# Attention visits on one core: an fp32 mask, one turn for two blocks, small transposes held for the turn, and one fill per visit

## The chip, the cores and the metric

The kernel runs on one core of a Trainium2 chip. The metric is the device time of one execution in microseconds (us). Five engines work side by side: TensorE (PE in the profile; its weight loads are PEld), VectorE (DVE), ScalarE (ACT), GpSimd (POOL) and SyncE (SP), which issues transfers.

## The reference: a decoder trunk of two layers

The input is 512 tokens by 1024 features, float32. Layer 0 mixes by attention, layer 1 by a short gated convolution, and each layer ends in a gated MLP with a causal convolution of width 3 (2816 features). Only the attention of layer 0 matters here. It has 16 heads of 64: eight "forgetting" heads with a softmax, and eight "stick-breaking" heads.

```python
# forgetting heads, per block of 128 queries
logits = q @ k.T * scale + cum_f[query] - cum_f[key]
logits = where(key_pos <= q_pos, logits, -inf)
out    = softmax(logits) @ v
# stick-breaking heads
z       = q @ k.T * scale
later   = reverse_cumsum(where(strict, log_sigmoid(-z), 0)) - itself
out     = where(strict, exp(log_sigmoid(z) + later), 0) @ v
# both: heads concatenated, then o @ w_out, added to the residual
```

Queries and keys are normalized per head (`rms_norm`) before the product.

## The kernel before

Every product of two float32 matrices is made from halves: ScalarE rounds an operand to fp32r (`hi`, a copy), VectorE takes the rest (`lo`), and TensorE adds hi x hi, hi x lo and lo x hi in PSUM (`mm3`, lines 269 to 275). Weights come by DMA into `raw` and are split the same way (lines 250 and 251).

Attention works on eight pairs of heads; pairs 0 to 3 are forgetting heads (`fox`), 4 to 7 stick-breaking. A pair's 512 queries are four blocks of 128, handled in three units: blocks 0 and 1 together, block 2, block 3 (`UNITS`). So there are 24 visits, one per unit, and the loop at the end of the program runs over them (lines 901 to 916). In visit g:

- `logits(g)` puts the scores of unit g in two PSUM banks "b" (line 645; 64-row products, the two heads side by side). For forgetting heads it adds the decay with the rows `dr` and then the causal mask by a product of an identity with a 128 x 128 mask, both bf16 (line 654). Then softmax or the stick-breaking weights follow on VectorE and ScalarE (lines 662 to 668, 683 to 689) and leave the weights `w`.
- if unit g-2 was the last of its pair, `weigh` multiplies that pair's turned weights with the values (line 741) in banks "a".
- `turn` transposes the weights of unit g-1, block by block, on TensorE through the banks "c" (lines 705 and 717), and ScalarE and VectorE split them into `pt` hi and lo (lines 711, 712, 720, 721). There are two banks "c".

Between these steps stands filling work: generators in the list `fillers` that make one `mm3` (or one triple for values) at each step: projections of later queries and keys (`queries_keys`, lines 271 to 273), of values (`values`, lines 527 to 529), and the output projection (`output`, `output_begin`). `fill(us)` adds `us` to a quota and runs fillers until the quota is used up; if there are none, the quota is kept. `need(what)` calls `fill(0.5)` until something later work needs is there.

The planner's clock, `clock`, advances with `spend(us)`: 0.65 per `mm3`, and so on. `after(us, fn)` puts a small piece of work in the list `later`, and `spend` runs it once its time has come, in the middle of whatever is being written. Each pair's queries and keys have three such pieces: `sums` (3.0 after the second projection; 16 small products of line 564 into a bank "c"), `turned_sums` (1.5 later; two transposes of line 572 into the same bank, then the reciprocal root on VectorE) and `rows` (8.0 later; transposes of line 597, four for each of q and k that needs them, each four in a bank "c"; then line 599 multiplies and lines 372 and 373 split). Only then may that pair's scores be made.

The order so written isn't final: a scheduler of the compiler may put a later instruction ahead of one whose buffer isn't free by its own reckoning. Engines then run their instructions in the order that results.

The constants are `PRE` 12.0 (a fill ahead of the loop), `FILL1` 1.5 (behind the scores), `FILL2` 3.3 (behind the turn, shared between blocks) and `BEFORE` 2.0 (once, when the last scores have been made).

Of the kernel before, what the change touches and what calls it, by code (L numbers as in the profile page):

```python
# [17 lines left out]
F32 = mybir.dt.float32  # L18
F32R = mybir.dt.float32r
# [6 lines left out]
P = 128  # L26
S = 512
# [16 lines left out]
ORDER = (1, 0, 1, 1, 1, 1, 3)  # L44
SUMS, FLAT, ROWS = 3.0, 1.5, 8.0
NSUMS, NROWS, LATE = 4.0, 3.0, 7.0
FILL1, FILL2, BEFORE = 1.5, 3.3, 2.0
UNITS = (0, 1), (2,), (3,)
CLASSIC = 3
SHARE = 0.58  # L50
# [3 lines left out]
def trunk(  # L54
# [7 lines left out]
    act, dve, pe, pool = nc.scalar, nc.vector, nc.tensor, nc.gpsimd  # L62
# [10 lines left out]
    def bank(tag):  # L73
        n_ps[0] += 1
        return ps.tile([P, S], F32, tag=tag, name=f"ps{tag}{n_ps[0]}", bufs={"a": 2, "b": 4, "c": 2}[tag])
# [52 lines left out]
    ident16 = begin[:, S - P:S]  # L128
    make_identity(nc, ident16)
    mask = const.tile([P, P], BF16, tag="mask", name="mask")  # L130
# [51 lines left out]

    clock, later, fillers, quota = [0.0], [], [], [0.0]

    def spend(us):
        clock[0] += us
        while later and later[0][0] <= clock[0]:
            later.pop(0)[2]()

# [8 lines left out]
    def fill(us):  # L198
        quota[0] += us
        while quota[0] > 0 and fillers:  # L200
            before = clock[0]
            if next(fillers[0], None) is None:
                fillers.pop(0)
            quota[0] -= clock[0] - before
# [240 lines left out]
    def choose():  # L445

        one = const.tile([P, 4, 4], F32, tag="one", name="one")
        pool.memset(one, 0.0)
        for j in range(4):
            for e in range(2):  # L450
                pool.affine_select(
                    out=one[:, j, :], in_=one[:, j, :], pattern=[[-1, 4]], compare_op=ALU.not_equal,
                    fill=1.0, base=-(e * HD + 4 * j), channel_multiplier=1,
                )
        both = const.tile([P, 2, 4], F32, tag="both", name="both")
        pool.tensor_tensor(both, one[:, 0::2, :], one[:, 1::2, :], op=ALU.add)
        two = const.tile([P, 4, 2], F32, tag="two", name="two")
        pool.tensor_tensor(two, one[:, :, 0:2], one[:, :, 2:4], op=ALU.add)
        by = const.tile([P, 4], F32, tag="by", name="by")
        pool.tensor_tensor(by, two[:, :, 0], two[:, :, 1], op=ALU.add)  # L460
        cols = const.tile([P, 4], F32, tag="cols", name="cols")
        pool.tensor_tensor(cols[:, 0:2], by[:, 0:2], by[:, 2:4], op=ALU.add)
        pool.tensor_tensor(cols[:, 2:4], by[:, 0::2], by[:, 1::2], op=ALU.add)
        pool.tensor_scalar(cols[:, 3:4], cols[:, 3:4], -1.0, None, op0=ALU.mult)
        sel = {n: cols[:, i:i + 1] for i, n in enumerate(("hi", "lo", "q", "-k"))}
        for p in range(4):
            sel["q", p], sel["k", p] = (both[:, i, p:p + 1] for i in range(2))
        return sel
# [71 lines left out]
    def need(what):  # L540
        while what not in done:
            assert fillers
            fill(0.5)
# [75 lines left out]
    def at_once(u):  # L619

        return (slice(0, 2),) if u == 0 else (slice(0, 1), slice(1, 2))

    def logits(p, u):


        fox = p < 4
        need(("qk", p))
        need("decay")
        (k_hi, k_lo), (q_hi, q_lo) = (halves[p][i] for i in range(2))
        bs = UNITS[u]  # L630
        ss = [bank("b") for _ in range(2)]

        parts, at_ = [], 0
        for i, b in enumerate(bs):
            n = (b + 1) * P
            parts.append((b, n, 256 * i, at_))
            at_ += n
            spend((4 if fox else 3) * max(n, 256) * 0.00044 + (0.12 if fox else 0))

        def scores(ql, kl, first, last):  # L640
            for b, n, c, _ in parts:
                wide = max(n, 256)
                for e in range(2):
                    rows = slice(e * HD, (e + 1) * HD)
                    pe.matmul(ss[e][:, c:c + wide], ql[rows, b * P:n], kl[rows, 0:wide], start=first and b == bs[0], stop=last and b == bs[-1])  # L645

        scores(q_hi, k_hi, True, False)
        scores(q_hi, k_lo, False, False)
        scores(q_lo, k_hi, False, not fox)
        if fox:  # L650
            scores(dl[:, p, :], dr, False, False)
            for e in range(2):
                for b, n, c, _ in parts:
                    pe.matmul(ss[e][:, c + b * P:c + n], ident16, mask, start=False, stop=b == bs[-1])
        w = aw.tile([P, 2, S], F32, tag="w", name=f"w{p}{u}", bufs=2)
        own = [w[:, :, a:a + n] for b, n, c, a in parts]
        if fox:
            m = len(bs)
            top, total, inv = (tiny.tile([P, m, 2], F32, tag=f"{t}{m}", name=f"{t}{p}{u}") for t in ("top", "total", "inv"))
            for j, (b, n, c, a) in enumerate(parts):  # L660
                for e in range(2):
                    dve.reduce_max(top[:, j, e:e + 1], ss[e][:, c:c + n], axis=AX.X, negate=True)
                    act.activation(own[j][:, e, :], ss[e][:, c:c + n], AF.Exp, bias=top[:, j, e:e + 1], accum_out=total[:, j, e:e + 1])
            for es in at_once(u):
                dve.reciprocal(inv[:, :, es], total[:, :, es])
                for j in range(m):
                    for e in range(es.start, es.stop):
                        dve.tensor_scalar(own[j][:, e, :], own[j][:, e, :], inv[:, j, e:e + 1], None, op0=ALU.mult)
        else:

            scale = q_scale[p]
            if not rests:
                rests.append(aw.tile([P, 2, S + 1], F32, tag="rest", name="rest", bufs=1))
                pool.memset(rests[0][:, :, S:S + 1], 0.0)
            rest = rests[0]
            if u == 0:
                pool.memset(rest[:, :, P:P + 1], 0.0)
            for es in at_once(u):
                for j, (b, n, c, a) in enumerate(parts):
                    end = P if b == 0 else S  # L680
                    keys = slice(end - n, end)
                    for e in range(es.start, es.stop):
                        act.activation(rest[:, e, keys], ss[e][:, c:c + n], AF.Sigmoid, scale=scale[:, 1, b, e:e + 1])
                        act.activation(own[j][:, e, :], ss[e][:, c:c + n], AF.Sigmoid, scale=scale[:, 0, b, e:e + 1])
                        back = rest[:, e, keys][:, ::-1]
                        dve.tensor_tensor_scan(back, back, begin[:, S - n:S][:, ::-1], 0.0, op0=ALU.mult, op1=ALU.max)  # L686
                for j, (b, n, c, a) in enumerate(parts):
                    end = P if b == 0 else S
                    dve.tensor_tensor(own[j][:, es], own[j][:, es], rest[:, es, end - n + 1:end + 1], op=ALU.mult)
        return [(b, x) for (b, n, c, a), x in zip(parts, own)]  # L690
# [87 lines left out]
    def output_begin():  # L778
        last_w.append([weights(), weights(AHEAD - 1)])
        yield from output_part(range(4), range(2), "b")  # L780
        last_w.append([weights(AHEAD - 1), weights(0)])
        yield from output_part(range(4), (2,), "b")
# [96 lines left out]
    aw = attn.enter_context(tc.tile_pool(name="aw", bufs=2))  # L879
# [4 lines left out]
    o_tiles = {0: mixed(0)}  # L884

    dl = ap_.tile([P, 4, S], F32R, tag="dl", name="dl")
    dr = aw.tile([P, 2, S + 1], F32, tag="rest", name="dr", bufs=1)[:, 0, 0:S].bitcast(F32R)
    sel = choose()
    run(qk0)
    load_small()  # L890
# [7 lines left out]
    units = [(p, u) for p in range(8) for u in range(len(UNITS))]  # L898
    waiting = {}
    fill(PRE)  # L900
    for g in range(len(units) + 2):
        if g < len(units):
            waiting[g] = logits(*units[g])
            fill(FILL1)
        if g == len(units):
            fillers.append(output_begin())
            fill(BEFORE)
        if g >= 2 and units[g - 2][1] == len(UNITS) - 1:
            p = units[g - 2][0]
            weigh(p)  # L910
            if p == 3:
                fillers.append(output(0, residual))
        if 1 <= g <= len(units):
            for b, w in waiting.pop(g - 1):
                turn(units[g - 1][0], b, w)
                fill(FILL2 / len(UNITS[units[g - 1][1]]))
    fill(1e9)

    def residual_out(o, acc, nxt):
# [668 lines left out]
```

## Time and profile before

| | us |
|---|---|
| median of 3 runs (lowest, highest) | 1141.16 (1140.47, 1141.63) |
| the profiled execution, its time | 1140.43 |
| its span, first to last instruction | 1138.5 |
| mean granted TensorE clock | 0.998 |

The page gives each engine's busy time and its share of the span; the window view does the same for a stretch. In rows in order of time, the first number is the start in us from the span's beginning, the second the length from the first to the last of the merged instructions, `x4` their count, and a bracket at the end tells how long the engine had been idle and who ended that. A matmul's length includes the array's latency, so consecutive ones overlap in the record: what one costs is the distance to the next one's start. A by-form row gives the count, busy us and mean ns of one, then the idle time before them. Engine names are followed by the line of the kernel.

### The profile page before, as it was taken

To read this page: it belongs to the slowest core of one execution; us is meant where nothing else is said; L and a number is where in the kernel's file an instruction comes from. 1 tells how busy PE (TensorE), PEld (TensorE's weight loads), DVE (VectorE), ACT (ScalarE), POOL (GpSimd) and SP (SyncE) were. 2 spreads that over 40 slices of the span, in tenths; PEclk is the share of its full clock that TensorE was granted. 3 is DMA by queue.
4 is the path that set the end of the run, shared out by engine and by line. 5 is a ranking of instruction groups with operands and counts; after the bars stand their busy time and mean duration, and the time that the engine had idled before them with its cause. 6 is when DMAs were issued, how large, how long until landed. Compare 5 with 4: busy or idle time off the path is not lost.

```text
span 1138.5 us, 19066 instructions
## 1 busy us (share of the span) xinstructions
PE 1123.4 (99%) x7547; PEld 1006.6 (88%) x7547; DVE 959.3 (84%) x1453; ACT 669.3 (59%) x999; POOL 136.0 (12%) x150
## 2 busy tenths in 40 slices
PE   8999999999999999999999999999999999999998
PEld 6888787878889999999999899988889999998776
DVE  5787888887899899989788889865898898989775
ACT  7556576755545667676475455543445767676553
POOL 4000000000012111014400001000012111014400
PEclk9999999999999999999999999999999999999999
DMA  6412212022366877689944555543275867699952
GB/s 192 112 38 75 56 39 73 26 87 75 110 178 120 179 170 162 173 247 190 213 101 143 145 144 133 113 118 98 83 192 117 191 161 162 172 246 190 206 144 83
DMA packets 161080, 155.31 MB, mean 136 GB/s; under 512 B 6396, under 2 KB 136492, under 8 KB 160992
## 3 DMA queue, kind: packets, MB, share of 16 engines
q1 hardware_dynamic: 124256, 106.94, 30.6%
q0 software_dynamic: 36576, 47.10, 25.8%
q8 instruction: 59, 0.97, 0.3%
q14 instruction: 29, 0.24, 0.1%
q10 hardware_dynamic: 160, 0.07, 0.0%
HBM read 149.10 MB, written 2.10 MB: 133 GB/s over the span
## 4 chain that ended last, share of the span: by engine, by line
PE 86%; DVE 8%; DMA 2%; ACT 2%; issue 1%; SPq 0%; DVEq 0%; ACTq 0%
PE psb L997 25%; PE psa L997 10%; PE psb L1505 10%; PE psb L271 6%; PE psb L272 6%; PE psb L273 6%; PE psa L1505 5%; PE psa L273 4%; PE psa L272 4%; PE psa L271 4%; DVE wlo L251 2%; DMA raw<-in_ffn_w_down 2%; PE psb L645 1%; PE psa L741 1%; DVE rest L686 1%
## 5 line engine op out<-in xcount | busy, mean ns | idle before, releaser
L250 ACT ACTIVATE whi<-raw 128x1024 fp32r<-128x1024 f32 (+2 forms) x97 | 100.0, 1033 | 110.2 <-PE psb L272 32.0
L251 DVE TENSOR_TENSOR wlo<-raw,whi 128x1024 fp32r<-128x1024 f32 (+2 forms) x97 | 115.2, 1189 | 41.4 <-ACT whi L250 39.4
L997 PE MATMUL psb<-p_hi,wlo_p 128*128 128x256 f32 x384 | 108.3, 282 | 0.6 <-DVE wlo_p L950 0.6
L997 PE MATMUL psb<-p_lo,whi_p 128*128 128x256 f32 x384 | 108.1, 281 | 0.0
L997 PE MATMUL psb<-p_hi,whi_p 128*128 128x256 f32 x384 | 107.8, 281 | 0.0
L271 PE MATMUL psb<-hs_a,whi 128*128 128x512 f32 x256 | 104.6, 409 | 0.0
L273 PE MATMUL psb<-hs_a,wlo 128*128 128x512 f32 x256 | 101.3, 397 | 0.0
L997 PEld LDWEIGHTS psb<-p_hi,wlo_p 128*128 128x128 f32 x384 | 72.2, 188 | 0.8 <-DVE wlo_p L950 0.8
L997 PEld LDWEIGHTS psb<-p_hi,whi_p 128*128 128x128 f32 x384 | 72.8, 190 | 0.0
L997 PEld LDWEIGHTS psb<-p_lo,whi_p 128*128 128x128 f32 x384 | 72.2, 188 | 0.0
L997 PE MATMUL psa<-p_lo,whi_p 128*128 128x256 f32 x256 | 72.0, 281 | 0.0
L997 PE MATMUL psb<-q_hi,whi_q 128*128 128x256 f32 x256 | 72.0, 281 | 0.0
L997 PE MATMUL psb<-q_lo,whi_q 128*128 128x256 f32 x256 | 72.0, 281 | 0.0
L997 PE MATMUL psb<-q_hi,wlo_q 128*128 128x256 f32 x256 | 72.0, 281 | 0.0
L997 PE MATMUL psa<-p_hi,wlo_p 128*128 128x256 f32 x256 | 72.0, 281 | 0.0
L997 PE MATMUL psa<-p_hi,whi_p 128*128 128x256 f32 x256 | 71.8, 281 | 0.0
L1505 PE MATMUL psb<-act,whi 128*128 128x256 f32 x352 | 63.0, 282 | 0.4 <-DVE act L950 0.4
L380 DVE SCALAR_TENSOR_TENSOR uv<-yv,taps,uv 128x511 f32<-128x511 f32 (+1 forms) x88 | 62.5, 745 | 0.2
L380 DVE SCALAR_TENSOR_TENSOR ug<-yg,taps,ug 128x511 f32<-128x511 f32 (+1 forms) x88 | 62.0, 743 | 0.3 <-ACT ug L377 0.3
L271 PEld LDWEIGHTS psb<-hs_a,whi 128*128 128x128 f32 x256 | 48.4, 189 | 10.7 <-issue 1.2
L273 PEld LDWEIGHTS psb<-hs_a,wlo 128*128 128x128 f32 x256 | 48.1, 188 | 10.9
L1505 PE MATMUL psb<-whi,act 128*128 128x512 f32 x176 | 57.4, 399 | 0.1
(453 smaller groups left out, 3654.9 us busy)
## 6 DMA issues: line engine op xcount, KB each, us to landing
raw<-in_attn_w_in SPq DMA_DIRECT2D x24, 512.0 KB, 4.0
raw<-in_ffn_w_up SPq DMA_DIRECT2D x24, 512.0 KB, 3.9
raw<-in_ffn_w_down SPq DMA_DIRECT2D x20, 512.0 KB, 8.1
X<-in_ffn_w_up SPq DMA_DIRECT2D x16, 512.0 KB, 4.7
W<-in_ffn_w_up SPq DMA_DIRECT2D x16, 512.0 KB, 6.7
Y<-in_ffn_w_up SPq DMA_DIRECT2D x16, 512.0 KB, 4.6
Z<-in_ffn_w_up SPq DMA_DIRECT2D x16, 512.0 KB, 4.9
Y<-in_ffn_w_up POOLq DMA_DIRECT2D x16, 512.0 KB, 9.8
```

Source lines behind the costliest of these rows:

```text
L250: return (act.activation(hi[:, at_], raw[:, at_], AF.Copy), dve.tensor_tensor(lo[:, at_], raw[:, at_], f32(hi[:, at_]), op=ALU.subtract))
L251: dve.tensor_tensor(lo[:, at_], raw[:, at_], f32(hi[:, at_]), op=ALU.subtract))
L271: made = [pe.matmul(acc, w[0], rhs[0], start=first, stop=False), pe.matmul(acc, w[0], rhs[1], start=False, stop=False), pe.matmul(acc, w[1 ...
L272: pe.matmul(acc, w[0], rhs[1], start=False, stop=False),
L273: pe.matmul(acc, w[1], rhs[0], start=False, stop=last)]
L380: dve.scalar_tensor_tensor(dst[:, d:], src[:, 0:S - d], tap(j), dst[:, d:], op0=ALU.mult, op1=ALU.add)
L645: pe.matmul(ss[e][:, c:c + wide], ql[rows, b * P:n], kl[rows, 0:wide], start=first and b == bs[0], stop=last and b == bs[-1])
L686: dve.tensor_tensor_scan(back, back, begin[:, S - n:S][:, ::-1], 0.0, op0=ALU.mult, op1=ALU.max)
L741: pe.matmul(out_, w, t[:, first:first + step * (NB - k - 1) + 1:step, :], start=k == 0 and i == 0, stop=k == NB - 1 and i == 1)
L997: pe.matmul(to, w[a][:, k, c], x[b][:, k, :], start=fresh and i + k + t == 0, stop=i == 1 and k == 3 and t == 2, skip_group_check=not fresh)
L1505: pe.matmul(to, l, r, start=begin and o + t == 0, stop=end and t == 2 and o == (0 if layer else 1), skip_group_check=not fresh)
```

## The change

Four things change in attention.

- The mask product uses two 128 x 128 fp32r tiles, `above` (the mask) and `unit` (the identity), in place of the bf16 ones. They lie in the unused second half of the buffer that holds `dr`, and GpSimd copies them there once.
- The two blocks of a unit 0 are turned one behind the other, with no fill between.
- Small pieces in `later` get a grace: in the loop of visits `spend` runs one only when it is 4.0 overdue (`GRACE`). A new function, `gather`, runs all that are due, and is called ahead of the turn.
- The fill of 1.5 behind the scores goes; the one behind the turn is 4.8. The visit then reads: scores, weighing where there is one, gathering, turn, fill. Visit 0 has no fill.

```diff
-FILL1, FILL2, BEFORE = 1.5, 3.3, 2.0
+FILL2, BEFORE, GRACE = 4.8, 2.0, 4.0
...
+    grace = [0.0]
+
     def spend(us):
         clock[0] += us
+        while later and later[0][0] + grace[0] <= clock[0]:
+            later.pop(0)[2]()
+
+    def gather():
         while later and later[0][0] <= clock[0]:
             later.pop(0)[2]()
...
-                    pe.matmul(ss[e][:, c + b * P:c + n], ident16, mask, start=False, stop=b == bs[-1])
+                    pe.matmul(ss[e][:, c + b * P:c + n], unit, above, start=False, stop=b == bs[-1])
...
-    dr = aw.tile([P, 2, S + 1], F32, tag="rest", name="dr", bufs=1)[:, 0, 0:S].bitcast(F32R)
+    held_rows = aw.tile([P, 2, S + 1], F32, tag="rest", name="dr", bufs=1)
+    dr, above, unit = (held_rows[:, i, c:c + n].bitcast(F32R) for i, c, n in ((0, 0, S), (1, 0, P), (1, P, P)))
+    pool.tensor_copy(above, mask)
+    pool.tensor_copy(unit, ident16)
...
     fill(PRE)
+    grace[0] = GRACE
     for g in range(len(units) + 2):
         if g < len(units):
             waiting[g] = logits(*units[g])
-            fill(FILL1)
...
         if 1 <= g <= len(units):
+            gather()
             for b, w in waiting.pop(g - 1):
                 turn(units[g - 1][0], b, w)
-                fill(FILL2 / len(UNITS[units[g - 1][1]]))
+            fill(FILL2)
+    grace[0] = 0.0
     fill(1e9)
```

## The prediction, made before the changed kernel was run

> **What bounds the kernel now.** I read the page first, then the stretch of attention by windows, TensorE in order of time there, and last the waits. The page's busy times:
>
> ```profile
> PE 1123.4 (99%) x7547; PEld 1006.6 (88%) x7547; DVE 959.3 (84%) x1453; ACT 669.3 (59%) x999; POOL 136.0 (12%) x150
> ```
>
> TensorE is the bound, end to end: time appears only where it idles or where its instructions are further apart. The change touches attention alone, from the first scores to the last weighing (51.8 to 258.3 us). The windows view (length, then busy time and count of each engine):
>
> ```profile
> 51.80:258.30 206.50, 203.21 (x1383) 166.90 (x1383) 172.22 (x386) 130.76 (x275) 0.45 (x5) 1.00 0.21 58
> 51.80:155.00 103.20, 102.61 (x752) 84.72 (x752) 81.76 (x219) 65.85 (x151) 0.14 (x2) 1.00 0.22 57
> 155.00:258.30 103.30, 100.59 (x633) 82.18 (x632) 90.46 (x169) 64.92 (x125) 0.31 (x3) 1.00 0.20 59
> ```
>
> TensorE idles 206.50 - 203.21 = 3.3 us, of which 2.7 in the second half; no filling of gaps can gain more than that. VectorE is busy 83% of the stretch, so what is queued there comes late. The other reserve is what TensorE loses where it turns from one kind of work to another. Its rows in order of time (start, length, operation, count); the distance from a row to the next is what the row cost:
>
> ```profile
> 58.95 0.38 PE L705 MATMUL psc<-ident,w 128*128 128x128 f32 x2
> 59.09 0.48 PE L271 MATMUL psb<-hs_a,whi 128*128 128x512 f32 x1
> 59.40 0.40 PE L272 MATMUL psb<-hs_a,whi 128*128 128x512 f32 x1
> 59.63 0.40 PE L273 MATMUL psb<-hs_a,wlo 128*128 128x512 f32 x1
> ...
> 64.33 0.29 PE L654 MATMUL psb<-mask,begin 128*128 128x128 bf16 x2
> 64.42 0.48 PE L271 MATMUL psb<-hs_a,whi 128*128 128x512 f32 x1
> 64.74 0.40 PE L272 MATMUL psb<-hs_b,whi 128*128 128x512 f32 x1
> ...
> 65.89 1.03 PE L597 MATMUL psc<-ident,qwide 128*128 128x128 f32 x8
> 66.68 0.48 PE L271 MATMUL psb<-hs_a,whi 128*128 128x512 f32 x1
> 67.00 0.40 PE L272 MATMUL psb<-hs_b,whi 128*128 128x512 f32 x1
> ```
>
> A steady 512-column product takes 59.63 - 59.40 = 0.23. Eight transposes take 66.68 - 65.89 = 0.79, and the first product behind them 0.32 in place of 0.23, so 0.88 in all, 0.11 each. Two transposes take 0.14 + (0.31 - 0.23) = 0.22: again 0.11 each. A break between transposes and filling work is therefore nearly free, whatever its length. That is the main reading: fewer, longer stretches have almost nothing to save on TensorE itself.
>
> **The change part by part.** (a) The mask. 32 mask products: four visits with four (two blocks by two heads), eight with two. Now they stream in bf16 between scores and filling; afterwards in fp32 between scores and transposes.
>
> ```profile
> 72.51 0.39 PE L645 MATMUL psb<-dr,dl 64*128 64x256 f32 x4
> 72.83 0.40 PE L654 MATMUL psb<-mask,begin 128*128 128x128 bf16 x4
> 73.04 0.36 PE L527 MATMUL psb<-whi,hs_a 128*128 128x256 f32 x1
> 73.24 0.28 PE L528 MATMUL psb<-wlo,hs_a 128*128 128x256 f32 x1
> 73.36 0.28 PE L529 MATMUL psb<-whi,hs_b 128*128 128x256 f32 x1
> ```
>
> The weight loads, those of the mask (shortest, median, longest in ns) and of four short fp32 products in a weighing:
>
> ```profile
> L654 PEld LDWEIGHTS <-begin x32: 95/98/99, 53.5 to 142.9; 128*128 128x128 bf16 x32
> ...
> 83.08 0.53 PEld L741 LDWEIGHTS psa<-pt,v 128*128 128x128 f32 x4
> ```
>
> Now a group of four costs 0.21 plus the late first product behind it, 0.20 - 0.12 = 0.08: 0.29. A group of two costs 64.42 - 64.33 = 0.09, plus 0.32 - 0.23 = 0.09: 0.18. In fp32 each product must have its own weight load, and where short fp32 products follow each other those loads set the pace: the four loads in the L741 row span 0.53, less the last one's 0.19 is 0.34 for three, 0.11 each. So four cost 0.45 and two 0.23 (with a trifle for the first transpose behind them): 4 x (0.45 - 0.29) + 8 x (0.23 - 0.18) = 0.64 + 0.40 = 1.0 us; I take +1.0. Below: if the loads hid entirely, a 128-column product still streams as long as the bf16 one, so 0.0; a gain is excluded, as the columns are the same. Above: 32 x (0.11 - 0.05) = +1.9. The Trainium skill ("TensorE: Matmul & The Clock Gate", sections on LDWEIGHTS and on fast weight load) says that weights load fast only when they aren't FP32 and that otherwise a load takes the columns over 1.2, an estimate of 107 ns for 128. That speaks against this edit, and the trace agrees (0.11 us); by it the sum would be 32 x (107 - 56) ns = +1.6 us.
>
> (b) Turning straight behind the scores. Where no mask stands between (the stick-breaking visits, eight without a weighing), scores now meet transposes instead of filling.
>
> ```profile
> 149.86 0.40 PE L645 MATMUL psb<-qk_hi,qk_lo 64*128 64x256 f32 x4
> 150.19 0.39 PE L527 MATMUL psb<-whi,hs_a 128*128 128x256 f32 x1
> 150.41 0.28 PE L528 MATMUL psb<-wlo,hs_a 128*128 128x256 f32 x1
> ...
> 71.10 0.28 PE L645 MATMUL psb<-qk_lo,qk_hi 64*128 64x256 f32 x2
> 71.48 0.65 PE L564 MATMUL psc<-sq,head_ones 128*32 128x128 f32 x16
> 72.05 0.39 PE L645 MATMUL psb<-qk_lo,qk_hi 64*128 64x256 f32 x2
> ```
>
> To filling: 0.33 for two pairs of scores, less one steady pair of 0.12, is 0.21, and 0.10 lost on the next product: 0.31. To other fp32 work from the same scores: 0.38. So about +0.07 for each, half of them with longer scores where the difference is smaller: taken +0.3 (-0.3 to +0.6). Fewer breaks and the joint turn of two blocks: some 40 breaks by about 0.01, -0.3 (0 to -0.4).
>
> (c) Held small work. The 16 sums of squares (L564) cost 0.57 where they cut into other work, against 4 x 0.11 for themselves, with 0.26 to get in (0.38 - 0.12) and about 0.10 to get back: nearly 0.5 lost. Directly behind scores, ahead of transposes, 0.2 of that is saved. By the code's own clock two of seven land there (pairs 1 and 7); the rest still go off by GRACE in a fill, in `need` or in a weighing. -0.4 (0 to -1.4). The other small transposes are of the kind that breaks for free.
>
> (d) PSUM banks "c". There are two. A sum's bank is held until its own transposes are read; these wait for the next gathering now, a visit instead of 1.5 us. Then the turn's two groups share one bank, and each needs ScalarE and VectorE before the bank is free, both queued behind the softmax just issued. Before shows such a case:
>
> ```profile
> 192.60 0.82 PE L717 MATMUL psc<-ident,w 128*128 128x128 f32 x6
> 194.37 0.91 ACT L720 ACTIVATE pt<-psc 128x384 fp32r<-128x384 f32 x2
> 196.95 1.01 DVE L721 TENSOR_TENSOR pt<-psc,pt 128x384 fp32r<-128x384 f32 x2
> 197.56 0.66 PE L597 MATMUL psc<-ident,qwide 128*128 128x128 f32 x4 [1.32 <-DVE pt L721]
> ```
>
> The low halves left VectorE 5 us after the transposes, and TensorE stood 1.3 us. On the other hand the compiler's scheduler doesn't keep the written order: when a bank is late, a turn comes out in two parts with filling between. The rows of one turn of six in before:
>
> ```profile
> 67.47 0.55 PE L717 MATMUL psc<-ident,w 128*128 128x128 f32 x3
> ...
> 68.22 0.49 PE L717 MATMUL psc<-ident,w 128*128 128x128 f32 x3
> ```
>
> Three value products stand in the place of the dots, and no idle time. So most collisions become another order, not a wait. Net of the 3.3 us of idle time that exists: +0.5 (-3 to +5).
>
> (e) Late rows. By the code's clock (0.65 per triple of products) pair 1's second projection ends at 10.4 after the first fill. Before, its rows come out at 24.6 and the scores that need them at 30.0. After, the first fill ends at 12.4, two scores add 1.1 and 0.8, and sums go at the gathering at 14.3 (0.6 of their own); their transposes, due 1.5 later at 16.4, go only at 21.1 with GRACE, so rows are due 8 after these, at 29.4, and with GRACE again leave at 33.8, inside `need`, with the scores of pair 1 at once behind them; pair 3 likewise. The chain between is two products on VectorE, a split on ScalarE and VectorE:
>
> ```profile
> L599 DVE TENSOR_TENSOR qn<-qk,psc 128x512 f32<-128x512 f32 x10 | 6.7, 680 | 1.0 <-PE psc L597 0.9
> L372 ACT ACTIVATE qk_hi<-qn 128x512 fp32r<-128x512 f32 x10 | 6.2, 628 | 9.0 <-DVE qn L599 9.0
> L373 DVE TENSOR_TENSOR qk_lo<-qn,qk_hi 128x512 fp32r<-128x512 f32 x10 | 6.7, 689 | 2.2 <-ACT qk_hi L372 2.1
> ```
>
> 2 x 0.68 + 0.63 + 0.69 = 2.7 us, twice. The cover is a turn and 4.8 us of filling, if the scheduler draws them ahead: +0.5 (0 to +5.4).
>
> (f) The end. `need` adds 0.5 to the quota at each try: 13 and 10 tries, 11.5 us of filling spent early. So the last filling (output_begin) is used up before the last turn, and the last weighing follows that turn with nothing between.
>
> ```profile
> 251.48 1.03 PE L717 MATMUL psc<-ident,w 128*128 128x128 f32 x8
> 252.11 1.09 ACT L720 ACTIVATE pt<-psc 128x512 fp32r<-128x512 f32 x2 [3.79 <-PE psc L717]
> 252.74 1.29 DVE L721 TENSOR_TENSOR pt<-psc,pt 128x512 fp32r<-128x512 f32 x2 [1.41 <-ACT pt L720]
> 255.82 2.65 PE L741 MATMUL psa<-pt,v 128*128 128x512 f32 x16
> ```
>
> The first head's low half is ready about 252.74 + 0.65, 1.9 us after the turn began, and the turn itself takes 0.8. Uncovered: +1.1 (0 if the next output products are drawn ahead, to +2.0 with the wait behind the weighing).
>
> At no cost: two small copies on GpSimd early (idle there in this stretch but for 0.45 us); mask and unit in the "rest" buffer are last read with `dr`, well before stick-breaking takes it.
>
> Sum: 1.0 + 0.3 - 0.3 - 0.4 + 0.5 + 0.5 + 1.1 = +2.7 us on the profiled execution, which took 1140.43 (span 1138.5). The median of the runs is 1141.16, 0.7 above it; the forecast on that scale is 1143.9, say 1144.0.
>
> **The rivals.** A measurement can tell about 0.2% (2.3 us) from no change.
> Faster: the cause would be one, the second half's 2.7 us of idle time vanishing because filling always stands behind the turn, where the banks are being emptied. With -2.8 for idle time, -1.4 for sums held, -0.3 for breaks, +0.3 for the mask and nothing for (b), (e), (f): -4.2, so 1137.0. For it: the longest single wait above, 1.32, is for L721. Against: the first half has only 0.6 us to give, and the bank is held longer, not shorter. It decides if the held transposes find both banks free; chance 0.22.
> No change: the scheduler breaks the joint turn and pulls filling in wherever something is late, as it does now, and only mask and small terms remain: +0.5 to +2, 1141.5 to 1143. This is also the case in which the change doesn't do what it says. Chance 0.28.
> Forecast, a little slower (1143.4 to 1148): 0.37.
> Much slower: banks starve. With one bank for a turn in some six of eight pairs and half of the 1.32 us above at each of its two groups, 12 x 0.7 = +8, and the rows of pairs 1 and 3 uncovered, +4: 1153. Against it: VectorE still has 17% free. Chance 0.13.
>
> **How the numbers follow.** Faster 0.22, same 0.28, slower 0.37 + 0.13 = 0.50. The range reaches into both outer cases, leaving about one in ten on each side: 1137.5 to 1151. The likeliest case alone spans 1143.4 to 1148.
>
> **What would show it.** In the profile after, the L654 loads should read near 190 ns in fp32, and a group of four mask products should cost 0.4 us or more: if it stays at 0.2 to 0.3, (a) is wrong. The stretch of attention should have 4 to 6 us of idle TensorE; under 2 speaks for the faster rival, over 8 for starving banks, and the waits view must then name L597, L705 or L717 as waiting for pt. The last L717 x8 should be followed by L741 with a gap of about 1 us; if output products stand between, (f) is wrong. Scores of pair 1 directly behind an L597 x8 with a gap would show (e). I am wrong altogether if the time falls while the idle time stays: then a price of turning between kinds of work exists that the distances above don't show.

## The result and the profile after

The changed kernel takes 1150.37 us (median of 4 runs, 1148.97 to 1150.49) against 1141.38 (4 runs of before): 9.0 us slower, ratio 1.008, 95% interval 1.0064 to 1.0096. The profiled execution took 1150.49 with a span of 1148.3.

The first line is the page of the changed kernel, the busy times as in the prediction's first fence.

```profile
PE 1129.0 (98%) x7547; PEld 1010.0 (88%) x7547; DVE 959.3 (84%) x1453; ACT 670.1 (58%) x999; POOL 136.4 (12%) x152
```

The count of products is the same. To see where the time went I took a stretch that holds the same work in every kernel: from the transposes of the decay, just ahead of attention, to those of the next norm. The windows view of it, before and after (length, busy us and count by engine):

```profile
43.93:293.06 249.13, 245.84 (x1573) 201.34 (x1572) 205.32 (x440) 152.46 (x306) 0.45 (x5) 1.00 0.22 62
```

```profile
43.31:303.68 260.37, 251.98 (x1576) 204.77 (x1575) 205.45 (x440) 153.22 (x306) 0.44 (x5) 1.00 0.21 59
```

The stretch is 11.2 us longer; 1.4 of that comes back outside it, 0.6 of this by an earlier start. TensorE's idle time rose from 249.13 - 245.84 = 3.3 to 260.37 - 251.98 = 8.4, so 5.1 of the 11.2 are plain waits. The other 6.1 are TensorE "busy" longer with the same products: rows further apart.

The mask is one part of that. TensorE in order of time, after, a group of four and what follows; then the loads of all 32 by the view of their line:

```profile
104.92 0.40 PE L651 MATMUL psb<-dr,dl 64*128 64x256 f32 x4
105.24 0.66 PE L660 MATMUL psb<-dr 128*128 128x128 f32 x4
105.74 1.06 PE L723 MATMUL psc<-ident,w 128*128 128x128 f32 x8
106.56 0.48 PE L277 MATMUL psb<-hs_a,whi 128*128 128x512 f32 x1
```

```profile
L660 PEld LDWEIGHTS psb<-dr x32: 186/189/192, 52.3 to 159.4; 128*128 128x128 f32 x32
```

The group takes 0.50 where it took 0.21, and its loads 189 ns where they took 98. The eight transposes behind it take 0.82 to the next product, where eight took 0.79 before: breaks between transposes and filling stayed nearly free. With all filling counted as one kind of work, the rows of the stretch fall into 173 groups of one kind before and 154 after. That is 19 breaks fewer, and no gain shows.

The largest waits of TensorE, by what ended them (us in all, times, longest), first before and then after:

```profile
PE psc L597 <- DVE pt L721: 1.3, 1, 1.3
PE psc L564 <- DVE pt L721: 1.1, 2, 0.7
```

```profile
PE psa L747 <- DVE h L793: 1.6, 1, 1.6
PE psa L747 <- DVE o L754: 1.3, 1, 1.3
PE psc L711 <- DVE pt L718: 1.2, 1, 1.2
PE psc L723 <- DVE qn L605: 0.9, 2, 0.5
PE psc L723 <- DVE pt L727: 0.9, 2, 0.5
PE psc L711 <- DVE qn L605: 0.7, 1, 0.7
```

Four of these six lines are turns (L711, L723) that wait for a bank "c", by the low halves `pt` or by the rows' product `qn`: 3.7 us. The other two, 2.9 us, are weighings (L747) that wait for a bank "a", which VectorE empties late; such waits took 0.7 before, and no run here changes the banks "a". The turn of the third line, with the engines that empty the banks:

```profile
114.87 0.64 PE L570 MATMUL psc<-sq,head_ones 128*32 128x128 f32 x16
...
116.77 0.41 PE L711 MATMUL psc<-ident,w 128*128 128x128 f32 x2
...
117.23 0.59 ACT L613 ACTIVATE sq<-psb 128x512 f32<-128x512 f32 x1
...
117.71 0.69 ACT L621 ACTIVATE qk<-psb,head_gains 128x512 f32<-128x512 f32 x1
...
118.42 0.59 ACT L753 ACTIVATE o<-psa 64x512 f32<-64x512 f32 x1
118.64 0.39 PE L278 MATMUL psb<-hs_a,whi 128*128 128x512 f32 x1
119.04 0.38 ACT L717 ACTIVATE pt<-psc 128x256 fp32r<-128x256 f32 x1
...
119.77 0.42 DVE L718 TENSOR_TENSOR pt<-psc,pt 128x256 fp32r<-128x256 f32 x1
...
120.25 0.66 PE L711 MATMUL psc<-ident,w 128*128 128x128 f32 x4 [1.21 <-DVE pt L718]
```

The first block's two transposes stand at 116.77, but ScalarE comes to them at 119.04, behind the square and the scaled copy of a later projection (L613, L621) and a weighing's output (L753), and VectorE at 119.77. The other bank is held by the sums of a later pair (L570 at 114.87), whose transposes wait for the next gathering and come at 123.07. So the second block of the "joint" turn comes 3.5 us behind the first, with filling between and 1.21 us of nothing.

A wait costs a little more than its idle time. From the row at 118.64 to the next one are 1.61 us; less a steady 0.23 that is 1.38, where the record shows 1.21. After has 12 such waits, before 5, so 7 x 0.17 = 1.2 of the 6.1 us are an estimate of this. The mask takes some 2.6 (the first run below). The remaining 2.3 or so lie in scores, turns and weighings, and were not traced further.

### The profile page after: what moved, and what is told of

It is laid out like the page before. It is cut to its first block, busy times and chain, and to the rows that moved or that the text cites. A ratio compares the mean times of both kernels' runs of the same rounds, so it can differ in the third digit from the quotient of the medians.

```text
span 1148.3 us, 19070 instructions
## 1 busy us (share of the span) xinstructions
PE 1129.0 (98%) x7547; PEld 1010.0 (88%) x7547; DVE 959.3 (84%) x1453; ACT 670.1 (58%) x999; POOL 136.4 (12%) x152
## 4 chain that ended last, share of the span: by engine, by line
PE 87%; DVE 7%; ACT 3%; DMA 3%; issue 1%; DVEq 0%; ACTq 0%
PE psb L1008 24%; PE psb L1516 10%; PE psa L1008 9%; PE psb L279 6%; PE psb L277 6%; PE psb L278 6%; PE psa L1516 5%; PE psa L279 4%; PE psa L278 4%; PE psa L277 4%; DMA raw<-in_ffn_w_down 2%; DVE wlo L257 2%; PE psb L651 2%; PE psa L747 1%; PE psc L723 1%
```

## The experiments

Each was timed beside the kernel before, whose medians were 1140.6 to 1140.9 there; a run's time is the median of 4 to 11 executions. "Stretch" is the length of the window above, in the one execution that was profiled; before it is 249.1, after 260.4. Line numbers move a little with each run's edit.

| run | what it is | us | over before (95% interval) | stretch | idle in it |
|---|---|---|---|---|---|
| e1_mask | before, fp32 mask alone | 1143.32 | +2.6 (1.6 to 3.9) | 251.9 | 3.6 |
| e2_bf16 | the change with the bf16 mask | 1149.03 | +8.3 (6.4 to 9.2) | 257.7 | 8.1 |
| e3_held | before, held small work alone | 1147.99 | +7.3 (5.7 to 8.6) | 258.0 | 5.4 |
| e4_one | before, joint turn and one fill behind it | 1145.77 | +5.1 (3.4 to 6.3) | 254.4 | 7.8 |
| e5_joint | before, joint turn alone | 1144.79 | +4.2 (2.6 to 5.7) | 253.0 | 5.3 |
| e5b_stretch | before, one fill behind the turn, blocks apart | 1143.81 | +3.2 (1.7 to 4.0) | 252.6 | 5.7 |
| e6_free | the change, sums' bank free at once | 1146.70 | +6.1 (4.1 to 7.1) | 256.4 | 5.5 |
| e7_quota | the change, early filling taken from the quota | 1156.13 | +15.5 (13.8 to 17.0) | 265.1 | 9.3 |
| e8_sums | before, the sums alone held | 1145.32 | +4.6 (2.5 to 5.6) | 253.8 | 5.8 |
| e9_own | before, sums' transposes in a bank of their own | 1141.47 | +0.7 (-0.5 to 1.5) | 249.1 | 3.3 |
| e10_held_own | e3_held with that bank | 1145.25 | +4.5 (3.0 to 5.8) | 254.4 | 4.7 |
| e11_ahead | before, joint turn and one fill ahead of it | 1143.05 | +2.2 (1.4 to 3.5) | 251.4 | 3.6 |

**The mask (e1_mask, e2_bf16).**

```diff
-                    pe.matmul(ss[e][:, c + b * P:c + n], ident16, mask, ...)
+                    pe.matmul(ss[e][:, c + b * P:c + n], unit, above, ...)
```

e2_bf16 undoes the same line, and the buffer, in the changed kernel.

> The kernel before with the fp32 mask alone, order and fills unchanged. Theory A (weight loads set the pace of the mask products, TensorE being the bound): a group of four takes about 0.5 us and a group of two 0.28, as in the changed kernel; less the late first product behind a bf16 group, which goes, that is +1.7 to +2.0 us on the whole: about 1143.2. Rival (the bookkeeping of TensorE's distances misleads, other waits absorb it): no change within 0.6 us. The prediction's own price was +1.0.

> The changed kernel with the bf16 mask back, nothing else undone. Theory A: about 2 us under the changed kernel, 1148.3, so that some 7 us of the loss stay and belong to the order of the work. Rival (the mask is the main cause, because its longer stretch also delays the softmax that follows): most of the loss goes, 1144 or less.

+2.6 for e1_mask. In the changed kernel the bf16 mask gives back 1.3 by the medians, 0.7 with each over its own before (9.0 to 8.3), and 2.6 by the stretch (260.4 to 257.7); the two times aren't clear of each other's intervals, so the size rests on e1_mask. The order is unchanged there (the same 173 groups), so its cost can be read row by row. TensorE in order of time, e1_mask, the group of two that the prediction showed at 64.33:

```profile
64.33 0.44 PE L654 MATMUL psb<-dr 128*128 128x128 f32 x2
64.61 0.44 PE L271 MATMUL psb<-hs_a,whi 128*128 128x512 f32 x1
64.89 0.40 PE L272 MATMUL psb<-hs_b,whi 128*128 128x512 f32 x1
```

0.28 in place of 0.09, and the first product behind it is still late, 0.28 in place of 0.32 (steady 0.23): +0.15. The groups of four give 0.50 against 0.21, less the same 0.04: +0.25. 8 x 0.15 + 4 x 0.25 = 2.2 us. That the mask is the main cause falls: with the bf16 mask the change still loses 8.3 (6.4 to 9.2).

**Held work and one stretch apart (e3_held, e4_one).**

```diff
+    grace[0] = 4.0        # e3_held, with gather() ahead of the turn
...
-            fill(FILL1)                              # e4_one
...
-                fill(FILL2 / len(UNITS[units[g - 1][1]]))
+            fill(FILL1 + FILL2)
```

> The kernel before with the held small work alone: gathering ahead of the turn, a grace of 4.0 in the loop, the two fills and the separate blocks as they were, bf16 mask. Theory H (holding keeps a bank c occupied and brings rows late, and that starves the turn): +4 us or more, near 1145.5, with waits for bank c by pt or qn of 3 us or more in sum. Theory S (the cause is the turn put straight behind the scores, ahead of all filling): within 1.5 us of before.

> The kernel before with one fill of 4.8 behind a joint turn, nothing held, bf16 mask. Theory S (turn, softmax and what is left of the small work now ask ScalarE and VectorE at the same moment): +4 us or more, near 1145.5, with new waits of TensorE for pt. Theory H: within 1.5 us of before. If each gives about half, the two add up.

Each theory got the time it asked for, +7.3 and +5.1, so neither excludes the other. Theory H did not get its sign: in e3_held the waits for a bank "c" come to 1.3 us, all by `qn` and none by `pt`, where it asked for 3. Theory S got a new wait for `pt` (L597 for L712, 1.1 us). With the mask the parts add to 15.0, the whole is 9.0, so the parts don't add. e3_held has the smaller idle time of the two and loses more: its TensorE is busy 6.8 us longer than before. Its rows show a part of that (L650 scores, L710 a turn, L746 a weighing):

```profile
231.35 0.50 PE L650 MATMUL psb<-qk_hi,qk_hi 64*128 64x512 f32 x2
231.69 0.39 PE L650 MATMUL psb<-qk_lo,qk_hi 64*128 64x512 f32 x1
232.01 0.66 PE L710 MATMUL psc<-ident,w 128*128 128x128 f32 x4
232.59 0.50 PE L650 MATMUL psb<-qk_lo,qk_hi 64*128 64x512 f32 x1
233.03 1.50 PE L746 MATMUL psa<-pt,v 128*128 128x512 f32 x8
...
235.89 0.50 PE L650 MATMUL psb<-qk_hi,qk_lo 64*128 64x512 f32 x2
```

One unit's scores come in three pieces. Every entry into the 64-row scores costs two tenths: 0.34 from the first row here to the next, where 0.23 is steady, and 0.33 in place of 0.23 for the last 512-column product ahead of it. Leaving them costs about as much again, by the prediction's rows. The groups of scores in the stretch went from 27 to 33; at 0.4 each, six more are an estimate of 2.4 us. The rest of the 6.8 was not traced. In the changed kernel the groups of scores number 27 as before, so there this isn't the cause.

**The two halves of e4_one (e5_joint, e5b_stretch).** e5_joint calls `fill(FILL2)` once behind both blocks; e5b_stretch drops `fill(FILL1)` and shares 4.8 between the blocks.

> The kernel before with the joint turn alone: both blocks of a unit 0 one behind the other, then the same 3.3 of filling; fill of 1.5 behind the scores kept. Theory A (a break between transposes and filling is free, and two free banks c stand ready): no change, within 0.8 us of before. Rival (two blocks at once take both banks c and hold up the small work): +1.5 to +3.

> The kernel before without the fill behind the scores, 4.8 behind the turn and still shared between the blocks. Theory S (what costs is the turn straight behind the scores): +4 to +5, like the joint turn and the one fill together, which took +5.1. Rival (it was the joint turn that cost): within 1.5 us of before.

Neither is harmless, neither is the whole: +4.2 and +3.2, together +5.1. "No change" for the joint turn was wrong, and e5b_stretch lies between its two forecasts. The waits of e5_joint (L705 turns blocks 0 and 1):

```profile
PE psc L597 <- DVE pt L721: 1.7, 2, 1.3
PE psc L705 <- DVE qn L599: 1.3, 1, 1.3
PE psc L564 <- DVE pt L721: 1.3, 2, 0.7
```

The middle line is new: the rows of pair 5 had just taken one bank "c", the first block took the other, and the second block waited for `qn`. The first line has one more wait than before. With it the idle time grew by about 2 of the stretch's 3.9 us; the rest is spread over later groups and wasn't traced to one cause.

**The bank (e6_free, e9_own, e10_held_own).**

```diff
         def turned_sums(t, flat):
+            t = bank("c")
             for i in range(2):
                 pe.transpose(t[:, (2 + i) * P:(3 + i) * P], flat[:, i * P:(i + 1) * P], ident)
```

> The changed kernel, with the two transposes of the sums in a bank c of their own, so that the bank of the sums is free as soon as ScalarE has copied it and isn't held till the next gathering. Theory H (the held bank starves the turn): 2 to 3 us under the changed kernel, and the waits of transposes for pt and qn, 3.7 us in sum, at most 1.5. Rival (VectorE and ScalarE are late whatever the banks): within 1 us of the changed kernel, the waits stay.

> The kernel before with the transposes of the sums in a bank c of their own and nothing else. Theory H (two banks c, one of them held by the sums, are what the small waits of before come from): 0.5 to 2 us under before, 1139 to 1140.2. Rival (the bank was held only 1.5 us of the planner's clock here, which is harmless, and one more allocation is one more wait): no change or up to 1 us over.

> The kernel before with all small work held, as in the run that took +7.3, and the sums' transposes in a bank c of their own. Theory H (the held bank is the larger part): at most +4. Theory L (late rows cut scores in two and the bank matters little): +5.5 or more, with groups of scores still cut by turns.

With this line the changed kernel gets back some 3 to 4 us (1150.4 to 1146.7; each over its own before, 9.0 to 6.1; the stretch 260.4 to 256.4), and the kernel with held work alone 2.8 (the stretch 3.6). The waits of e6_free:

```profile
PE psa L748 <- DVE h L794: 1.6, 1, 1.6
PE psa L748 <- DVE o L755: 1.3, 1, 1.3
PE psc L712 <- DVE qn L606: 0.7, 1, 0.7
PE psc L724 <- DVE qn L606: 0.5, 1, 0.5
PE psc L712 <- ACT flat L573: 0.4, 2, 0.2
```

Those for a bank "c" fell from 3.7 to 1.6, of which 1.2 are for `pt` and `qn`, within the 1.5 of theory H; the time fell by a little more than its 2 to 3. Those of the weighings for a bank "a" stayed, to the tenth. The turn shown above, in e6_free:

```profile
117.04 0.41 PE L712 MATMUL psc<-ident,w 128*128 128x128 f32 x2
...
117.65 0.66 PE L712 MATMUL psc<-ident,w 128*128 128x128 f32 x4 [0.20 <-ACT flat L573]
```

The second block comes 0.61 us behind the first instead of 3.5, as soon as ScalarE has copied the sums out of the other bank. So the held bank is shown. It is a good third of what holding costs alone (2.8 of 7.3): e10_held_own at +4.5 is neither the at most +4 of theory H nor the +5.5 of theory L, so the bank isn't the larger part. In e9_own, without holding, TensorE's groups are those of before and the time is the same: there the bank was no burden, and the hope of a faster kernel fell.

**What of the small work must not be held (e8_sums).** A list of its own for `sums`, with the grace; their transposes and the rows go when due.

> The kernel before, holding the sums of squares alone for the gathering (with the grace of 4.0); their transposes and the rows go off when due, as before. Theory L (of the 7.3 us that holding all three took, the most comes of rows that are late for the scores that need them, since grace is paid three times over): at most +2.5. Rival (delaying the chain's head is enough, or the sums are at the wrong place there): +5 or more.

+4.6 lies between the two: more than half of e3_held's loss comes already with the head of the chain. But each piece is timed from the one before it, so holding the head makes the rows late too, and the run can't tell the two apart. Its waits do name late rows:

```profile
PE psb L659 <- ACT qk_hi L386: 1.7, 4, 0.6
...
PE psc L611 <- DVE qwide L604: 0.7, 1, 0.7
```

Four times the scores (L659) wait for the split of rows just made, and once the rows' transposes (L611) wait for their input: 2.4 us, none of it in before. TensorE's idle time rose by 2.5 in all; the rest of the stretch's 4.6 us are rows further apart, not traced.

**The quota (e7_quota).**

```diff
     def need(what):
         while what not in done:
-            fill(0.5)
+            before = clock[0]
+            if next(fillers[0], None) is None:
+                fillers.pop(0)
+            quota[0] -= clock[0] - before
```

> The changed kernel, with the filling that a missing pair's rows call for taken from the quota instead of added to it, so that filling isn't used up ahead of the last turn. Theory of the end (early use costs the cover of the last weighings): 0.5 to 1.5 us under the changed kernel, and output products between the last eight transposes and the last weighing. Rival (the waits in the middle are all that counts): within 0.5 us.

Both times were wrong: 5.8 us slower than the change. The sign of the first theory came: output products stand between the last eight transposes (265.44) and the last weighing (271.19). But the filling that `need` brings forward is then missing behind the next turns. In the stretch TensorE idles 9.3 us, and turns wait for the rows, the softmax and `pt`:

```profile
PE psc L726 <- DVE qn L608: 2.0, 4, 0.9
PE psc L714 <- DVE rb_qk L372: 1.6, 1, 1.6
PE psc L714 <- DVE w L698: 1.3, 3, 0.6
PE psc L726 <- DVE pt L730: 1.2, 1, 1.2
```

That is only 0.9 more idle time than in the change; the other 3.9 us of the longer stretch are rows further apart, and weren't traced. So the growing quota, which I had put down as a loss at the end, pays in the middle by the time; what it buys there is not shown.

**The place of the one stretch (e11_ahead).** `fill(FILL1 + FILL2)` between scores and a joint turn, nothing behind the turn but 3.3 behind the last one.

> The kernel before with one fill of 4.8 per visit put ahead of a joint turn, between scores and turn (behind the last turn 3.3, to cover the last weighing); bf16 mask, nothing held. Theory S (one stretch is harmless, but a turn straight behind the scores meets their softmax on ScalarE and VectorE): within 1.5 us of before, or under it. Rival (a turn with no filling behind it is followed by scores whose softmax then meets the turn's splits, and joint turns want both banks c at once, so one stretch costs wherever it stands): +3 to +5, like the stretch behind the turn.

+2.2, neither near zero nor near the +5.1 of the same stretch behind the turn. The waits are gone (3.6 us idle, before 3.3, against 7.8 behind the turn), so it is the place of the stretch that makes them. That a turn straight behind the scores meets their softmax is a reading; no wait of e4_one names the softmax. What is left may lie again in cut scores: 32 groups in place of 27, an estimate of 2.0 us at 0.4 each. No version beat the kernel before.

## Why the prediction was right, and where its terms were off

The direction and the range were right: slower, 1150.4 in 1137.5 to 1151.0. The size was not: the forecast was +2.7, measured +9.0, between the likeliest case (to 1148) and the rival of starving banks (1153). That 1150.4 lies in the range, 0.6 under its end, is owed to the range's reach into that rival, not to the sum: the mask, the joint turn and the one stretch were priced too low and holding had the wrong sign. The prediction's own sign for the rival came too: idle time over 8 us (8.4), with turns that wait for `pt` (L711, L723).

- **TensorE is the bound, and breaks are free.** Right between transposes and filling: 19 breaks fewer bought nothing that shows, and eight transposes take 0.82 to the next product, before 0.79. Breaks at the 64-row scores do cost, some 0.4 a group.
- **(a) The mask, +1.0 with a limit of +1.9.** Measured +2.6 alone, 2.2 from its rows. The mechanism was right, the products follow each other at the pace of their loads, 0.11. The mis-sized step: I let the late first product behind the group go to nothing, and put no price on the group's start. The product stayed late (0.28 against 0.23), and the first mask product behind the scores takes 0.16 in place of 0.11 (0.50 for four, where 4 x 0.11 is 0.45). These two, 0.05 each for 12 groups, are the 1.2 between 1.0 and 2.2. The limit counted loads alone, and was too low for the same reason. The Trainium skill ("TensorE: Matmul & The Clock Gate", section on LDWEIGHTS) gives the columns over 1.2 for a load, an estimate of 107 ns for 128. The trace agrees with that as the pace (0.11 us), though the record of one load reads 189 ns.
- **(b) Turning straight behind the scores, +0.3, and the joint turn as a saving of 0.01 per break.** Both steps failed. As a matter of TensorE's switching they hold: after, the last 256-column scores ahead of a turn take 0.21 and the first transpose 0.16 in place of 0.11, no more than leaving for filling costs. But the joint turn also asks for two banks at once, which was priced nowhere in (b): +4.2 alone. And the missing fill behind the scores was priced as a switch only: +3.2 alone.
- **(c) Holding, -0.4.** Failed in sign: +7.3 alone, and 1149.0 - 1145.8 = +3.3 on top of the one stretch. No run prices the saving for sums next to scores by itself.
- **(d) Banks "c", +0.5 of a range to +5.** The mechanism named, a bank held from one gathering to the next, is the one that e6_free takes away: 3 to 4 us. I took a small value since the scheduler reorders. It did so, but TensorE then runs the order as it stands: behind the row at 118.64 the second block comes ahead of the last product of a triple, which runs only at 120.66, and TensorE stood still.
- **(e) Late rows, +0.5.** Seen, and small. TensorE after, at pair 1:

```profile
77.97 0.66 PE L603 MATMUL psc<-ident,qwide 128*128 128x128 f32 x4
78.47 0.66 PE L723 MATMUL psc<-ident,w 128*128 128x128 f32 x4
79.59 0.66 PE L723 MATMUL psc<-ident,w 128*128 128x128 f32 x4 [0.46 <-DVE qn L605]
80.06 0.49 PE L747 MATMUL psa<-pt,v 128*128 128x512 f32 x1
80.58 0.50 PE L651 MATMUL psb<-qk_hi,qk_hi 64*128 64x256 f32 x4
```

The rows (L603) are there just ahead of the scores, as worked out, and the turn covers most of the chain; a weighing's first product was drawn in too. Pair 3 looks alike (rows at 138.08, scores at 140.57), without a wait there. Where the sums alone were held, e8_sums, late rows show as 2.4 us of waits.

- **(f) The end, +1.1.** The order came as worked out, the price didn't:

```profile
270.15 1.03 PE L723 MATMUL psc<-ident,w 128*128 128x128 f32 x8
271.44 3.03 PE L747 MATMUL psa<-pt,v 128*128 128x512 f32 x16 [0.25 <-ACT pt L726]
```

The weighing follows the last turn with nothing between, 1.29 us behind its start instead of the turn's own 0.8: 0.5, not 1.1. It began on the high half and didn't wait for the low one. And the early use of filling that leads there isn't a loss on the whole: e7_quota, where the end is covered, is 5.8 us slower.

What remains open: some 2 us of the joint turn, the longer distances of rows where small work is held, and the waits for a bank "a". No run separates the grace from the gathering. Apart from e1_mask, each slower order differs from before in many places, and no run changed one of them by itself.

## What to carry to other kernels

Price a break between kinds of work by the distance of rows before spending an edit on having fewer: here transposes cost 0.11 us each in twos and in eights. An order that was fitted to two buffers has its filling where the buffers are being emptied, and here moving a short step next to others that use the same buffers cost more than the step; ask of each held piece which bank it keeps while it is held, and what starts later because of it. Parts that each lose may lose less together, so the sum of the parts is no forecast, and a cheap edit (one bank freed early) can tell a theory from its rival.

## What the runs showed of the hardware that was not expected

A 128 x 128 product in fp32 straight behind 64-row products stands 0.16 us ahead of the second, where the following ones are 0.11 apart. This holds for the 12 mask groups of e1_mask and for the turns straight behind scores alike; in bf16 the first took 0.07 and the others 0.06. That the first weight load then has nothing to hide behind would explain it, but the records don't show it.

Of the kernel: a weighing could start 0.6 us earlier than I had worked out, since its first products need only the high half.
